# Three small reorderings in a Strassen MLP kernel: sums spread over three slots of a period, a reordered head, a last quarter by row tiles

## Chip, core and metric

The kernel runs on one core of one Trainium2 chip. The metric is the device time of one execution in microseconds. Every kernel below gave correct results. Times of one kernel agree within about 0.3% as a rule.

## The reference

```python
x (16, 512, 768)  w1 (768, 3072)  b1 (3072)  w2 (3072, 768)      # float32, random normal
y = x @ w1 + b1
y = 0.5 * y * (1 + erf(y / sqrt(2)))
return y @ w2
```

## The kernel before

Rows are taken in eight super-blocks of 1024. Each product is done by the Winograd form of Strassen's method: seven products of half-size blocks in place of eight, paid for by 16-bit sums of operands on VectorE. The second product of the last six super-blocks uses two levels of it. A super-block from the third on has twelve "periods" of the first product (`Unit1`), 4.53 us each, then seven of the second (`Unit3`), 6.93 us each. TensorE writes seven small products p1 to p7 into PSUM banks X, Y, Z and W; VectorE and ScalarE copy and add between the banks.

A period is one fixed order of work for the new unit `i` and the one before it, `j`. `fill(slot)` is where other work is pushed into the engines' in-order queues:

```python
def period(i, j, fill):
    ...                                    # [cut: the change from Unit1 to Unit3]
    p1(i); copy_xy(i)                      # X bank; ScalarE copies X to Y
    p7(j)                                  # onto j's Y bank; VectorE: Y add ("c22")
    fill(1)
    p5(i)                                  # W bank; ScalarE copies it out
    fill(2)
    p3(j)                                  # onto Z bank; VectorE: Z add ("c12")
    fill(3)
    p6(i)                                  # onto i's Y bank: needs copy_xy(i) done; then Y to Z copy
    j.right_done()                         # ScalarE: GELU of 1024 columns, needs the Z add
    fill(4)
    p4(j)                                  # ScalarE: GELU of the Y bank
    fill(5)
    p2(i)                                  # ScalarE: GELU of the X bank
    fill(6)
```

The sums that later products need wait in a queue. A slot takes from it as far as a budget in nanoseconds goes:

```python
def fill_mm1(sb, k, slot):                 # first product, super-blocks 2 to 7
    if slot == 1:
        ...                                # [cut: puts sums into the queue]
        sums(900)
    if slot == 4:
        sums(1500)
    ...                                    # [cut: loads of x, w1, w2; slot 5 loads only]
```

Since both queues of work are first-in-first-out, a sum put ahead of the Z add delays the Z add, and with it ScalarE's GELU and everything behind that.

The head (x tiles 4 to 7 are the bottom rows; `spin` is dummy matmuls):

```python
nc.gpsimd.tensor_copy(out=xh_of(0, 4)[:, 0:1], in_=xf[:, 1, 0:1])   # POOL waits for x tile 1 ...
for t in range(4, 8): load_x(0, t)                                   # ... before it asks for tiles 4 to 7
...
for t in range(4, 8):
    if t == 6: p2(first)
    transpose_pe(0, t)                     # TensorE transposes, ScalarE copies PSUM to SBUF
    spin(2 if t < 7 else 6)
    if t % 2:                              # sums S1, S2, A21, S4 of the top or the bottom half
        x_sums(0, soon, slice((t - 5) * P, (t - 3) * P))
        for k in range(4 if t < 7 else 2): soon.pop(0)[1]()
```

The end: in the last unit p4 goes onto the Y bank, VectorE adds 384 columns, one 192 KB store follows. The two sums that close the quarter before it (`c22_sum`, each with a 384 KB store) stand in slots 2 and 3 of the last full period.

## Time and profile before

| | before |
|---|---|
| time, median of 3 runs before the change | 865.12 us |
| profiled execution (865.78 us): span | 864.0 us |
| PE busy; LDWEIGHTS busy | 99%; 65% |
| 6310 matmuls at their usual spacing | 844.6 us |
| stretched spacing after the first 20 us | 8.7 us |
| last matmul's start to the end | 4.6 us |

"Spacing" is from the start of one matmul to the start of the next: 216 ns for 512 columns, 82 ns for 192, taken as the median of the trace. A "gap" below is what one spacing has beyond that. Gaps are the right measure here: the Trainium skill ("Perfetto Trace Analysis", Identifying the Most-Contended Engine) says that matmul busy share does not tell how close a kernel is to its limit, since matmuls are pipelined.

The timeline of the kernel before in a first-product period (columns: start us, busy us, engine, line, operation, output<-input, shapes, count, and in brackets idle time before it and what ended it). L179 is a sum, L562 the Z add, L386 and L391 GELUs, L528 the copy of X to Y.

```profile
593.11 1.21 DVE L179 TENSOR_TENSOR arena<-arena 128x512 f16<-128x512 f16 x3
...
594.24 0.68 DVE L562 TENSOR_TENSOR arena<-bZ,arena 128x512 f32<-128x512 f32 x1
...
595.49 1.15 ACT L386 ACTIVATE arena<-arena,b1t 128x1024 f16<-128x1024 f32 x1
...
597.11 0.69 ACT L391 ACTIVATE arena<-bX,b1t 128x512 f16<-128x512 f32 x1
...
597.68 0.60 ACT L528 COPY bY<-bX 128x512 f32<-128x512 f32 x1
...
598.34 1.46 PE L370 MATMUL bY<-arena 128*128 128x512 f16 x6
```

Three sums of slot 1 hold the Z add up to 594.24; ScalarE then works in a row to 598.28, and p6 starts at 598.34, with a gap of 275 ns. The timeline of the kernel before at the turn from the first product to the second and behind it. L535 is the Y add, L572 the "Z-bank add" of the second product (Y to Z), L462 its matmuls.

```profile
495.28 1.49 DVE L179 TENSOR_TENSOR arena<-arena 128x768 f16<-128x768 f16 x3
...
498.01 0.69 DVE L535 TENSOR_TENSOR arena<-bY,arena 128x512 f32<-128x512 f32 x1 [1.25 <-PE bY L370]
...
499.75 6.99 DVE L179 TENSOR_TENSOR arena<-arena 128x256 f16<-128x256 f16 x18
...
506.25 2.16 PE L462 MATMUL bY<-arena 128*128 128x192 f16 x24
...
509.17 0.57 DVE L572 TENSOR_TENSOR bZ<-bY,arena 128x384 f32<-128x384 f32 x1
...
517.05 0.56 DVE L572 TENSOR_TENSOR bZ<-bY,arena 128x384 f32<-128x384 f32 x1
...
517.66 1.15 PE L462 MATMUL bY<-arena 128*128 128x192 f16 x12 [0.35 <-DVE bZ L572]
```

VectorE idles 1.25 us before the Y add at 498.01, then has 18 sums to do.

The head of the kernel before, in its timeline: ScalarE's GELU and two transpose copies, the first bottom sum, p5 of the first unit, and p7 of the second unit, from which on the periods run steadily.

```profile
14.38 0.69 ACT L391 ACTIVATE arena<-bX,b1t 128x512 f16<-128x512 f32 x1 [0.26 <-PE bX L370]
...
14.96 1.49 ACT L296 COPY arena<-bT 128x768 f16<-128x768 f16 x2
...
16.48 1.62 DVE L179 TENSOR_TENSOR arena<-arena 128x768 f16<-128x768 f16 x3 [0.24 <-ACT arena L296]
...
17.10 0.81 PE L370 MATMUL bW<-arena 128*128 128x512 f16 x3 [0.42 <-DVE arena L179]
...
24.18 0.81 PE L370 MATMUL bY<-arena 128*128 128x512 f16 x3
```

Its last stretch (L179 with f32 are the two closing sums, L487 and L493 issue stores, L504 is the last add):

```profile
853.66 0.95 DVE L179 TENSOR_TENSOR arena<-arena 128x768 f32<-128x768 f32 x1
...
854.67 2.84 SPq L487 DMA_DIRECT2D out_dram<-arena  x4
...
858.45 1.15 PE L462 MATMUL bY<-arena 128*128 128x192 f16 x12
...
859.64 0.56 DVE L504 TENSOR_TENSOR arena<-bY,arena 128x384 f32<-128x384 f32 x1 [0.43 <-PE bY L462]
860.23 0.37 SPq L493 DMA_DIRECT2D out_dram<-arena  x1
```

### The profile page before, as it was taken

The page shows a single profiled execution, that of the slowest core. Times are in us where ns is not written, and L with a number is a line of the kernel's source. Part 1 is how long each engine was busy: PE and PEld are TensorE (multiplying, and loading weights), DVE is VectorE, ACT ScalarE, POOL GpSimd, SP SyncE. Part 2 cuts the span into 40 slices and gives each one's busy share as a digit, 9 for nine tenths or more (in the row PEclk, how much of TensorE's full clock was granted, in tenths as well). Part 3 has the DMA queues.
Part 4 walks back from the last instruction along what each step waited for, and adds up shares of the span by engine and source line. Part 5 has one row for each costly group of instructions (what it writes and reads, how often), then busy time and mean ns, then how long its engine had stood idle before and what let it go on. Part 6 is the DMA issues. An engine that isn't in the chain of part 4 may idle for free.

```text
span 864.0 us, 16201 instructions
## 1 busy us (share of the span) xinstructions
PE 853.0 (99%) x6310; PEld 560.9 (65%) x6310; DVE 653.7 (76%) x1106; ACT 420.6 (49%) x682; POOL 80.4 (9%) x131
## 2 busy tenths in 40 slices
PE   8999999999999999999999999999999999999997
PEld 4444445666544798448974499645995469944797
DVE  5765677656446998569976799667996689947997
ACT  5777762111178512874137732577216771277511
POOL 5111100000100001100020000200002100010000
PEclk9999999999999999999999999999999999999999
DMA  9987895659989698996989889897998959967397
GB/s 228 213 228 104 234 187 192 236 170 269 228 211 322 191 326 309 267 282 217 326 291 279 246 268 330 275 278 214 303 344 255 345 142 321 348 222 257 110 293 280
DMA packets 143249, 219.03 MB, mean 254 GB/s; under 512 B 61676, under 2 KB 84132, under 8 KB 143172
## 3 DMA queue, kind: packets, MB, share of 16 engines
q1 hardware_dynamic: 117952, 180.62, 66.1%
q0 software_dynamic: 25184, 37.36, 20.6%
q8 instruction: 49, 0.80, 0.4%
q14 instruction: 28, 0.23, 0.1%
q10 hardware_dynamic: 36, 0.01, 0.0%
HBM read 180.30 MB, written 47.87 MB: 264 GB/s over the span
## 4 chain that ended last, share of the span: by engine, by line
PE 82%; DVE 12%; issue 2%; DMA 2%; ACT 1%; SPq 0%; DVEq 0%; ACTq 0%
PE bY L370 21%; PE bX L370 14%; PE bY L462 10%; DVE arena L179 8%; PE bW L370 7%; PE bZ L370 6%; PE bX L462 6%; PE bY L410 5%; PE bX L410 4%; PE bZ L462 3%; PE bW L462 3%; PE bZ L410 2%; PE bW L410 2%; DMA arena<-w1s 1%; DVE bZ L572 1%
## 5 line engine op out<-in xcount | busy, mean ns | idle before, releaser
L179 DVE TENSOR_TENSOR arena<-arena 128x768 f16<-128x768 f16 (+4 forms) x620 | 393.8, 664 | 12.5 <-DMA arena<-arena 3.0
L370 PEld LDWEIGHTS <-arena 128*128 128x128 f16 x2016 | 196.3, 98 | 232.8 <-issue 3.5
L462 PEld LDWEIGHTS <-arena 128*128 128x128 f16 x3528 | 292.1, 98 | 12.6 <-issue 4.2
L370 PE MATMUL bY<-arena 128*128 128x512 f16 x864 | 218.9, 379 | 0.6
L535 DVE TENSOR_TENSOR arena<-bY,arena 128x512 f32<-128x512 f32 (+1 forms) x104 | 70.8, 681 | 149.6 <-PE bY L370 100.0
L528 ACT COPY bY<-bX 128x512 f32<-128x512 f32 (+1 forms) x146 | 80.3, 550 | 127.9 <-DVE arena L504 90.5
L370 PE MATMUL bX<-arena 128*128 128x512 f16 x576 | 141.5, 379 | 0.6 <-DMA arena<-w1s 0.6
L462 PE MATMUL bY<-arena 128*128 128x192 f16 x1512 | 139.8, 246 | 2.1 <-DVE bZ L572 2.1
L386 ACT ACTIVATE arena<-arena,b1t 128x1024 f16<-128x1024 f32 x96 | 110.3, 1149 | 57.5 <-DVE arena L562 57.5
L547 ACT COPY arena<-bW 128x512 f32<-128x512 f32 (+1 forms) x146 | 80.7, 553 | 95.5 <-PE bW L462 44.2
L410 PEld LDWEIGHTS <-arena 128*128 128x128 f16 x672 | 65.8, 98 | 44.2
L462 PE MATMUL bX<-arena 128*128 128x192 f16 x1008 | 92.0, 246 | 0.4
L562 DVE TENSOR_TENSOR arena<-bZ,arena 128x512 f32<-128x512 f32 (+1 forms) x104 | 70.5, 678 | 24.1 <-PE bZ L370 17.8
L370 PE MATMUL bW<-arena 128*128 128x512 f16 x288 | 77.8, 379 | 0.4 <-DVE arena L179 0.4
L370 PE MATMUL bZ<-arena 128*128 128x512 f16 x288 | 77.8, 379 | 0.0
L391 ACT ACTIVATE arena<-bX,b1t 128x512 f16<-128x512 f32 x96 | 65.3, 681 | 7.8 <-PE bX L370 7.8
L487 POOL DMA_DIRECT2D out_dram<-arena x42 | 30.5, 728 | 397.9 <-DVE arena L558 290.2
L391 ACT ACTIVATE arena<-bY,b1t 128x512 f16<-128x512 f32 x96 | 64.6, 673 | 0.0
L284 POOL DMA_DIRECT2D arena<-in_x_dram x60 | 32.3, 543 | 275.7 <-DMA arena<-arena 195.8
L577 DVE COPY bZ<-bY 128x512 f32<-128x512 f32 (+1 forms) x68 | 46.5, 683 | 6.7 <-PE bY L370 0.5
L410 PE MATMUL bY<-arena 128*128 128x384 f16 x288 | 49.6, 326 | 0.0
L462 PE MATMUL bW<-arena 128*128 128x192 f16 x504 | 49.0, 246 | 0.1
(41 smaller groups left out, 331.1 us busy)
## 6 DMA issues: line engine op xcount, KB each, us to landing
arena<-w2s SPq DMA_DIRECT2D x294, 288.0 KB, 4.6
arena<-w1s SPq DMA_DIRECT2D x72, 672.0 KB, 6.0
out_dram<-arena POOLq DMA_DIRECT2D x42, 384.0 KB, 5.1
w2s<-arena SPq DMA_DIRECT2D x49, 288.0 KB, 4.0
arena<-in_x_dram POOLq DMA_DIRECT2D x60, 192.0 KB, 6.8
w1s<-arena SPq DMA_DIRECT2D x12, 672.0 KB, 8.0
out_dram<-arena SPq DMA_DIRECT2D x21, 384.0 KB, 3.2
arena<-in_w_dram POOLq DMA_DIRECT2D x17, 384.0 KB, 8.1
```

The costliest lines, as they stand in the source:

```text
L179: nc.vector.tensor_tensor(out=o, in0=a, in1=b, op=op)
L284: nc.gpsimd.dma_start(out=xhs[t], in_=xr[:, sb * 8 + t, :])
L370: nc.tensor.matmul(out=dst[:, 0:RH], lhsT=w1_op(self.wt, slot)[:, c, :], rhs=a[:, c, :], start=first and c == 0, stop=c == self.C - 1, ski ...
L386: nc.scalar.activation(out=self.G[1][:, hi, :, :], in_=self.tmp, func=GELU, bias=b1t[:, 2 * hi + 1:2 * hi + 2])
L391: nc.scalar.activation(out=self.G[0][:, hi, row, :], in_=bank[:, 0:RH], func=GELU, bias=b1t[:, 2 * hi:2 * hi + 1])
L410: nc.tensor.matmul(out=dst[:, 0:N2], lhsT=a, rhs=w[:, :, c, :], start=first and c == 0, stop=c == self.C - 1, skip_group_check=True)
L462: nc.tensor.matmul(out=dst[:, t * N4:(t + 1) * N4], lhsT=a, rhs=w[:, c, :], start=first and c == 0 and t == 0, stop=c == NQ - 1, skip_grou ...
L528: nc.scalar.copy(out=bY[u.g % 2][:, 0:u.F], in_=bX[u.g % 2][:, 0:u.F])
L535: nc.vector.tensor_tensor(out=u.c22(), in0=bY[u.g % 2][:, 0:u.F], in1=w[:, 0:u.F], op=ADD)
L547: nc.scalar.copy(out=w[:, 0:u.F], in_=bW[:, 0:u.F])
L562: nc.vector.tensor_tensor(out=u.c12(), in0=bZ[:, 0:u.F], in1=w[:, 0:u.F], op=ADD)
L577: nc.vector.tensor_copy(out=bZ[:, 0:u.F], in_=bY[u.g % 2][:, 0:u.F])
```

## The change

Its intent: fewer sums ahead of the Z add; x's bottom rows asked for sooner and used sooner; a shorter piece of work behind the last matmul. The core of the diff, in three parts (cut: signatures that only pass the new arguments on).

```diff
 # --- sums ---
-                sums(900)
+                sums(500)              # slot 1
             if slot == 4:
                 sums(1500)
+            if slot == 5:
+                sums(500)

 # --- head ---
-        nc.gpsimd.tensor_copy(out=xh_of(0, 4)[:, 0:1], in_=xf[:, 1, 0:1])
+        nc.gpsimd.tensor_copy(out=xh_of(0, 4)[:, 0:1], in_=xf[:, 0, 0:1])
+        top, bottom = slice(0, 2 * P), slice(2 * P, RH)
         for t in range(4, 8):
-            if t == 6:
-                p2(first)
-            transpose_pe(0, t)
-            spin(2 if t < 7 else 6)
+            transpose_pe(0, t, nc.vector.tensor_copy if t == 5 else nc.scalar.copy)
             if t % 2:
-                x_sums(0, soon, slice((t - 5) * P, (t - 3) * P))
-                for k in range(4 if t < 7 else 2):
-                    soon.pop(0)[1]()
+                x_sums(0, soon, top if t == 5 else bottom, (0, 1))     # S1, S2 first
+                flush(soon)
+            if t < 7:
+                spin(2)
+        p2(first)
+        spin(3)
+        for r in (top, bottom):
+            x_sums(0, soon, r, (2,))
+        flush(soon)
+        for r in (top, bottom):
+            x_sums(0, soon, r, (3,))
-            on_act = isinstance(u, Unit3) or ...
+            on_act = u.g == 0 or isinstance(u, Unit3) or ...           # first unit's Y-to-Z copy by ScalarE
                 # [cut: both S4 sums are moved behind two sums of the next w1]

 # --- tail ---
+            def last(self, banks):                 # p4 of the last unit
+                for t in range(2):
+                    self.mm(4, banks[t], True, 0, self.C, (t,))
+                    o = self.dst[:, 1, t, 0, :]
+                    tt(o, banks[t][:, t * N4:(t + 1) * N4], o, ADD)
+                    nc.sync.dma_start(out=orr[:, self.sb * 8 + 2 + t, N2:N2 + N4], in_=o)
                 # [cut: the add of the Y bank moves up behind p7]
-                if sb + 1 == nsb and slot in (2, 3):
-                    units3[5].c22_sum(slot - 2)
+                if sb + 1 == nsb and slot in (1, 2):
+                    units3[5].c22_sum(slot - 1)
```

More of the change, by code (lines that the diff above doesn't have):

```diff
@@ L290, in transpose_dma, with transpose_pe @@
             nc.sync.dma_start_transpose(out=xT_of(sb, t), in_=xhs[t])
-        def transpose_pe(sb, t):
+        def transpose_pe(sb, t, copy=nc.scalar.copy):
             for kc in range(2 * KQ):
@@ L295, in transpose_pe @@
                                     identity=ident[:])
-            nc.scalar.copy(out=xT_of(sb, t), in_=bT[t % 2][:])
+            copy(out=xT_of(sb, t), in_=bT[t % 2][:])
         def blocks(sb):
@@ L300, in blocks, with x_sums @@
             return [XT[:, a, c:c + KQ, :] for a in range(2) for c in (0, KQ)]
-        def x_sums(sb, q, r=slice(0, RH)):
+        def x_sums(sb, q, r=slice(0, RH), ks=range(4)):
             A11, A12, A21, A22 = [a[:, :, r] for a in blocks(sb)]
@@ L305, in x_sums @@
             n = KQ * len(range(RH)[r])
-            later(n, lambda: tt(S1, A21, A22, ADD), q)
-            later(n, lambda: tt(S2, S1, A11, SUB), q)
-            later(n, lambda: tt(A21, A11, A21, SUB), q)
-            later(n, lambda: tt(S4, A12, S2, SUB), q)
+            ops = ((S1, A21, A22, ADD), (S2, S1, A11, SUB), (A21, A11, A21, SUB), (S4, A12, S2, SUB))
+            for k in ks:
+                later(n, lambda k=k: tt(*ops[k]), q)
         def g_sum(k, U, c0=0, c1=NH, q=None):
@@ L448, in __init__, with mm @@
                 self.alloc = lambda: None
-            def mm(self, q, dst, first, c0, c1):
+            def mm(self, q, dst, first, c0, c1, ts=(0, 1)):
                 A = OPERAND[self.p]
@@ L455, in mm @@
                 for c in range(NQ):
-                    for t in range(2):
+                    for t in ts:
                         r = slice(t * P, (t + 1) * P)
@@ L463, in mm @@
                                          rhs=w[:, c, :],
-                                         start=first and c == 0 and t == 0,
+                                         start=first and c == 0 and t == ts[0],
                                          stop=c == NQ - 1, skip_group_check=True)
                 load_ring(self.sb, n + RING)
+            def last(self, banks):
[4 more added lines that the diff above has]
+                    nc.sync.dma_start(out=orr[:, self.sb * 8 + 2 + t, N2:N2 + N4], in_=o)
             def quarter(self, o, r, h):
@@ L509, in finish @@
             def finish(self):
-                if self.ends:
-                    self.store_quarter(1, 0)
-                elif self.p in (2, 3, 4):
+                if not self.ends and self.p in (2, 3, 4):
                     self.store(0)
@@ L542, in p7 @@
                 u.store_quarter(1, 1)
+                u.left_done(1, bY[u.g % 2])
         def p5(u):
@@ L564, in p4 @@
         def p4(u):
+            if isinstance(u, Unit3) and u.ends:
+                u.last(bX)
+                return
             u.mm(4, bY[u.g % 2], False, 0, u.C)
@@ L569, in p6 @@
             u.mm(6, bY[u.g % 2], False, 0, u.C)
-            on_act = isinstance(u, Unit3) or (isinstance(u, Unit1) and u.sb >= ONE and u.g % 2)
+            on_act = u.g == 0 or isinstance(u, Unit3) or (isinstance(u, Unit1) and u.sb >= ONE and u.g % 2)
             if isinstance(u, Unit3) and u.add is not None:
@@ L718, in fill_a @@
             if slot == (1 if pos < at[1, 0] else 4) and pos + 1 < len(seq) and seq[pos + 1][0] == 0:
-                s4 = [soon.pop(1)] if pos == 0 else []
+                s4 = [soon.pop(0), soon.pop(0)] if pos == 0 else []
                 prep_wt(seq[pos + 1][1])
-                soon[3:3] = s4
+                soon[2:2] = s4
             if slot == 4:
```

## The prediction

> **What bounds it now.** The TensorE stream. The page shows PE busy 99% of the 864.0 us span at clock 0.999; VectorE is at 76%. In the timeline matmuls start 216 ns apart for 512 columns and 82 ns for 192; at such cadences 6310 matmuls take 844.6 us. So about 20 us is all that any reordering can touch: 4.9 us of stretched issue in the first 20 us, 8.7 us of later gaps, and head wait and tail.
>
> **First products (six super-blocks from 237 us).** PE's gaps end on ScalarE's copy of the X bank into the Y bank (about 197 ns at 371, 580 and 787 us; 277 ns at 598 and 806; 284 ns at 290, 498 and 706). The copy is late because two 16-bit sums (0.52 us each; three of 0.42) stand in slot 1 before VectorE's add of the Z bank, which then starts 0.4 to 0.5 us after its product ended; bank copy, three GELUs (1.15, 0.68, 0.68) and the X copy follow in a row. After: slot 1 holds one sum, the others go behind it or into slot 5, where VectorE idles 0.15 to 1.3 us. These eight gaps (2.0 us) should close. One 1024-column sum (0.68) also moves ahead of the batch of 18 at the change to the second product, so that batch ends earlier: the 187 and 101 ns gaps at 401/609/817 and 403/611/819 should close (0.85). Not touched: 511 ns before each "Z bank" add of the second product, six times (same order there), and the 730 ns wait for w1 at 387.
>
> **Head.** p5 of the first unit starts at 17.10, released by VectorE's last S1 sum, itself behind the last transpose copy (ScalarE busy with a GELU, two copies 14.96 to 16.45). After: that GELU comes after the copies, one copy goes to VectorE (estimate 0.9 us), sums stand S1, S2 first. I expect p5 near 16.3. Asking for x about 0.95 us sooner buys little: x tiles land at 11.57, 12.52, 13.51, 14.42, one each microsecond behind x and w1 already queued. The Trainium skill ("DMA: Bandwidth & Descriptors", Issuing engines are not separate DMA queues) says that all issuers share the same 16 engines; the trace agrees, about 380 KB/us read throughout. VectorE then is continuous (sums from 15.7, add, Z copy) until p7 of the second unit, near 23.6 instead of 24.18. Gain 0.55 us.
>
> **Tail.** Last matmul ends at 859.6; a 0.56 us add, then a 192 KB store 860.23 to 862.99. After: add of 192 columns (estimate 0.36), store of half the size; Most of the 2.8 us store is fixed. Gain 0.4 us.
>
> **Sum.** 2.85 + 0.55 + 0.4 = 3.8 us; I discount a little for gaps that move: 861.5 us, range 860.0 to 863.3. Chances: faster by over 2% 0.00, same 0.99, slower 0.01.
>
> **What would show it.** Gaps at the eight places and the two pairs gone, Z-bank add starting at its product's end; 511 ns gaps still there; first unit's p5 at 16.3; x bottom tiles landing no more than 0.4 us sooner; last store issued some 0.2 us earlier after the last matmul. Total PE excess after 20 us: 8.7 down to 5.5.
>
> **What would make it wrong.** Earlier x requests delaying w1's or x's first loads (p1 beyond 11.3); sums in slot 5 delaying the next Y add or Z copy, opening new gaps; waits for w1 reloads, which vary by run.

## More of the kernel before

From the page of the kernel before: its first line, the busy line, and the chain of waits that ended last, by engine.

```profile
span 864.0 us, 16201 instructions
...
PE 853.0 (99%) x6310; PEld 560.9 (65%) x6310; DVE 653.7 (76%) x1106; ACT 420.6 (49%) x682; POOL 80.4 (9%) x131
...
PE 82%; DVE 12%; issue 2%; DMA 2%; ACT 1%; SPq 0%; DVEq 0%; ACTq 0%
```

For 12% of the span the chain runs through VectorE, although VectorE is idle a quarter of the time.

## The result, and the profile after

The changed kernel took 858.08 us (857.61 to 858.25, 4 runs), the kernel before 865.15 us (4 runs): ratio 0.9915, 95% interval 0.9898 to 0.9933. (A ratio is the mean time of one kernel's fast runs over that of the other's of the same rounds, so it is not quite the ratio of the medians quoted.) That is "same" at a threshold of 2%, but it lies below the range that I gave: 7.1 us were gained, I had forecast 3.6.

The page of the kernel after, same lines:

```profile
span 856.2 us, 16201 instructions
...
PE 850.1 (99%) x6307; PEld 560.7 (65%) x6307; DVE 653.8 (76%) x1108; ACT 421.2 (49%) x682; POOL 80.6 (9%) x131
...
PE 97%; DMA 2%; ACT 0%; DVE 0%; SPq 0%; issue 0%
```

PE is busy 99% as before, and LDWEIGHTS rises only from 65% to 65.5% of a shorter span; what changed is the chain: VectorE's share of it fell from 12% to 0%. Where the 7.7 us between the two spans (863.97 and 856.25 us) came from, read off the two traces (the kernel before was profiled in an execution 0.6 us slower than its median; a gap of 39 ns near the end closed too):

| place | before | after | gained, us |
|---|---|---|---|
| eight gaps on the copy of X to Y (195 to 285 ns) | 1.99 us | 0.02 | 1.97 |
| three pairs of gaps at the turn to the second product (about 187 and 101 ns) | 0.86 | 0 | 0.86 |
| six gaps on the Z-bank add | 3.06 | 0.56 | 2.50 |
| two gaps at 45 and 49 us | 0.18 | 0 | 0.18 |
| p7 of the second unit starts at | 24.18 | 22.80 | 1.38 |
| last matmul's start to the end | 4.62 | 3.86 | 0.75 |
| wait for a reload of w1, at 387 us | 0.73 | 0.74 | 0 |

The first two rows, 2.83 us together, are what I had forecast (2.85). The third row was forecast as nothing, and the head and the tail came out larger.

The period of the kernel after at the same place in the schedule as the first one shown of before (L567 is the Z add, L390 a GELU, L532 the copy of X to Y):

```profile
589.43 0.41 DVE L179 TENSOR_TENSOR arena<-arena 128x512 f16<-128x512 f16 x1
...
589.76 0.68 DVE L567 TENSOR_TENSOR arena<-bZ,arena 128x512 f32<-128x512 f32 x1
...
592.64 0.69 ACT L390 ACTIVATE arena<-bX,b1t 128x512 f16<-128x512 f32 x1
...
593.21 0.60 ACT L532 COPY bY<-bX 128x512 f32<-128x512 f32 x1
...
594.03 1.46 PE L369 MATMUL bY<-arena 128*128 128x512 f16 x6
```

One sum, not three, stands ahead of the Z add, and the copy is over 0.22 us before p6 could start. The turn to the second product in the kernel after (L539 is the Y add, L580 the Z-bank add):

```profile
491.86 2.09 DVE L179 TENSOR_TENSOR arena<-arena 128x768 f16<-128x768 f16 x4
...
494.90 0.69 DVE L539 TENSOR_TENSOR arena<-bY,arena 128x512 f32<-128x512 f32 x1 [0.95 <-ACT arena L390]
...
496.64 6.26 DVE L179 TENSOR_TENSOR arena<-arena 128x256 f16<-128x256 f16 x17
...
502.86 2.14 PE L461 MATMUL bY<-arena 128*128 128x192 f16 x24
...
505.34 0.57 DVE L580 TENSOR_TENSOR bZ<-bY,arena 128x384 f32<-128x384 f32 x1
...
513.22 0.56 DVE L580 TENSOR_TENSOR bZ<-bY,arena 128x384 f32<-128x384 f32 x1
...
513.83 1.15 PE L461 MATMUL bY<-arena 128*128 128x192 f16 x12
```

Four sums instead of three run ahead of the Y add, in time in which VectorE was idle, and 17 are left behind it. From p6's first matmul to the first Z-bank add it is now 2.48 us, before it was 2.92; the second one holds TensorE up by 0.43 us less, too: its gap is 83 ns instead of 512.

The head of the kernel after, same lines as before, with ScalarE's Y-to-Z copy (L583):

```profile
14.51 0.80 ACT L296 COPY arena<-bT 128x768 f16<-128x768 f16 x1 [0.18 <-PE bT L294]
...
15.34 4.35 DVE L179 TENSOR_TENSOR arena<-arena 128x768 f16<-128x768 f16 x10 [0.87 <-ACT arena L296]
15.95 0.81 PE L369 MATMUL bW<-arena 128*128 128x512 f16 x3 [0.19 <-DVE arena L179]
...
17.44 0.57 ACT L583 COPY bZ<-bY 128x512 f32<-128x512 f32 x1
...
22.80 0.81 PE L369 MATMUL bY<-arena 128*128 128x512 f16 x3
```

A single copy stands between the last x tile and the first bottom sum, and ten sums then run on VectorE without a pause. The end of the kernel after (L472 issues the two halves of the last store):

```profile
846.00 0.95 DVE L179 TENSOR_TENSOR arena<-arena 128x768 f32<-128x768 f32 x1
...
847.01 3.27 SPq L493 DMA_DIRECT2D out_dram<-arena  x4
...
851.48 1.15 PE L461 MATMUL bX<-arena 128*128 128x192 f16 x12
...
852.17 0.85 DVE L179 TENSOR_TENSOR arena<-bX,arena 128x192 f32<-128x192 f32 x2
...
852.73 1.00 SPq L472 DMA_DIRECT2D out_dram<-arena  x2
```

### The profile page after: what moved, and what is told of

It is laid out like the page before. It is cut to its first block, busy times and chain, and to the rows that moved or that the text cites. A ratio compares the mean times of both kernels' runs of the same rounds, so it can differ in the third digit from the quotient of the medians.

```text
span 856.2 us, 16201 instructions
## 1 busy us (share of the span) xinstructions
PE 850.1 (99%) x6307; PEld 560.7 (65%) x6307; DVE 653.8 (76%) x1108; ACT 421.2 (49%) x682; POOL 80.6 (9%) x131
## 4 chain that ended last, share of the span: by engine, by line
PE 97%; DMA 2%; ACT 0%; DVE 0%; SPq 0%; issue 0%
PE bY L369 21%; PE bY L461 15%; PE bX L369 14%; PE bX L461 10%; PE bW L369 7%; PE bZ L369 7%; PE bY L409 5%; PE bZ L461 5%; PE bW L461 5%; PE bX L409 4%; PE bZ L409 2%; PE bW L409 2%; DMA arena<-w1s 1%; DMA arena<-in_x_dram 1%; PE bT L294 0%; ACT arena L296 0%
## 5 line engine op out<-in xcount | busy, mean ns | idle before, releaser
L539 DVE TENSOR_TENSOR arena<-bY,arena 128x512 f32<-128x512 f32 (+1 forms) x104 | 70.8, 681 | 144.7 <-PE bY L369 88.7
L532 ACT COPY bY<-bX 128x512 f32<-128x512 f32 (+1 forms) x146 | 80.3, 550 | 125.0 <-DVE arena L510 87.7
L567 DVE TENSOR_TENSOR arena<-bZ,arena 128x512 f32<-128x512 f32 (+1 forms) x104 | 70.7, 680 | 25.5 <-PE bZ L369 18.4
L390 ACT ACTIVATE arena<-bX,b1t 128x512 f16<-128x512 f32 x96 | 65.4, 681 | 7.5 <-PE bX L369 7.5
L390 ACT ACTIVATE arena<-bY,b1t 128x512 f16<-128x512 f32 x96 | 64.7, 674 | 0.0
L461 PE MATMUL bZ<-arena 128*128 128x192 f16 x504 | 48.5, 246 | 0.0
```

The lines of the kernel that those rows point to most:

```text
L390: nc.scalar.activation(out=self.G[0][:, hi, row, :], in_=bank[:, 0:RH], func=GELU, bias=b1t[:, 2 * hi:2 * hi + 1])
L461: nc.tensor.matmul(out=dst[:, t * N4:(t + 1) * N4], lhsT=a, rhs=w[:, c, :], start=first and c == 0 and t == ts[0], stop=c == NQ - 1, skip_ ...
L532: nc.scalar.copy(out=bY[u.g % 2][:, 0:u.F], in_=bX[u.g % 2][:, 0:u.F])
L539: nc.vector.tensor_tensor(out=u.c22(), in0=bY[u.g % 2][:, 0:u.F], in1=w[:, 0:u.F], op=ADD)
L567: nc.vector.tensor_tensor(out=u.c12(), in0=bZ[:, 0:u.F], in1=w[:, 0:u.F], op=ADD)
```

## The experiments

Eighteen kernels ran. All outputs are right. "Before" is the kernel before on the same chip.

### One part at a time, and one slot

`sums_only`, `head_only` and `tail_only` are the kernel before with one of the three parts of the diff. `no5_last` is the changed kernel with

```diff
-            if slot == 5:
+            if slot == 5 and k < NH - 1:
                 sums(500)
```

> The kernel before with only the sums spread over three slots. Backlog theory (VectorE enters the second product with one 0.68 us sum less to do, and carries no lateness to the Z-bank add): the six gaps of 511 ns shrink to about 80, the copy gaps (197, 277, 284 ns) and the 187/102 pairs close; time 5.0 to 5.6 us below the kernel before. Rival, the prediction's sum: the 511 ns gaps stay, 2.9 us below. Rival, that head or tail fed the gain: under 2 us below.

> The kernel before with only the head part. If the head is worth what the two traces show: p7 of the second unit near 22.8 us instead of 24.18, time 1.2 to 1.6 us below the kernel before; x's third tile and w1 land about 0.5 us sooner. Rival, that the sooner landing is a run-to-run matter: p7 near 23.3 to 23.6, 0.5 to 0.9 us below. The 511 ns gaps stay.

> The kernel before with only the last quarter by row tiles and the earlier closing sums. From the two traces: last matmul to end 3.8 us instead of 4.6, so 0.8 us below the kernel before (0.85 with the 39 ns gap closed). Prediction's estimate: 0.4 us. Nothing else moves.

> The changed kernel, with no sums in slot 5 of the twelfth (last) first-product period alone. Backlog theory: the moved 1024-column sum goes back behind the last Y add, VectorE is 0.68 us later into the second product, and TensorE loses about 0.6 us more in each of six super-blocks: 3.2 to 4.0 us above the changed kernel, the Z-bank gap back to 500 ns or more; the copy gaps stay closed. Rival (the lighter slot 1 of all periods did it): within 0.6 us of the changed kernel.

| kernel | median us (range) | before | ratio, 95% interval | gaps after 20 us in the trace |
|---|---|---|---|---|
| sums_only | 859.58 (859.04 to 860.86) | 864.73 | 0.9942 [0.9928, 0.9956] | 3.4 us (before: 8.7) |
| head_only | 866.48 (864.19 to 867.77) | 864.73 | 1.0015 [1.0001, 1.0028] | 8.2 us |
| tail_only | 865.23 (863.59 to 865.47) | 864.73 | 0.9997 [0.9985, 1.0010] | 8.6 us |
| no5_last | 861.98 (861.66 to 862.34) | 864.73 | 0.9965 [0.9953, 0.9978] | 6.8 us |

The sums alone give 5.2 us, with every Z-bank gap at 81 to 87 ns: the prediction's 2.9 us for this part is refuted. `no5_last` costs 3.9 us against the changed kernel: the copy gaps stay closed but for one of 175 ns at 388 us, while the pairs (about 188 and 102 ns, now in every super-block) and a Z-bank gap of 511 to 591 ns are back. So the third row of the table hangs on the one sum that slot 5 of the last period takes, not on the lighter slot 1.

Head and tail alone were misses: their traces show what was expected of them (p7 of the second unit at 23.1 us; 3.86 us from the last matmul to the end), yet the times do not.

### That slot alone; head and tail on top of the sums; a first attempt at a better version

`only5_last` is the kernel before with nothing but

```diff
+            if slot == 5 and k == NH - 1:
+                sums(500)
```

`sums_head` and `sums_tail` leave one part out of the change. `best` is the changed kernel with

```diff
-                sums(500)                              # slot 5
+                sums(1000 if k == NH - 1 else 500)
-                if 3 <= k < 11: transpose_dma(...)      # slot 3: ahead of the w1 and w2 loads
+                # the same in slot 5, behind them
-                    nc.sync.dma_start(...)              # both halves of the last store
+                    (nc.sync if t else nc.scalar).dma_start(...)
```

> The kernel before with one thing added: a slot of 500 ns of sums at the end of the twelfth first-product period, which pulls one 1024-column sum (0.68 us) ahead of the last Y add in each of six super-blocks. Backlog theory: the copy gaps (197, 277, 284 ns) stay, since slot 1 is as before; of the Z-bank gap and the 187/102 pair together 0.5 to 0.7 us per super-block go, so 3.0 to 4.2 us below the kernel before. Rival (light slot 1 did it): under 0.6 us below.

> The changed kernel without the tail part. Traces of the parts: head 0.6 us (p7 of the second unit comes 8.9 us after x's last tile lands instead of 9.1 to 9.8), so 858.6 to 859.1. If the parts interact as their separate runs seemed to (head alone 1.7 us above the kernel before): above 860.

> The changed kernel without the head part. The trace of the tail part alone says 0.75 us, so 858.6 to 859.0 here. If the parts interact (tail alone was no faster than the kernel before): above 859.4.

> A version meant to beat both: the changed kernel, with 1000 instead of 500 ns of sums in slot 5 of the last first-product period (closes the six gaps of 80 ns: 0.45 us), the x transposes of a period issued behind the loads of w1 and w2 (the 737 ns wait for w1 goes, and others like it in runs not profiled), and the first half of the last store issued by ScalarE (the second half is issued about 0.2 us sooner). Expected 856.4 to 857.4, against 858.1; if the w1 wait is the DMA engines' and not the queue's order, 857.4 to 857.8.

| kernel | median us (range) | before | ratio, 95% interval |
|---|---|---|---|
| only5_last | 861.22 (860.84 to 864.86) | 864.74 | 0.9959 [0.9946, 0.9972] |
| sums_head | 858.66 (857.73 to 862.54) | 864.74 | 0.9935 [0.9921, 0.9948] |
| sums_tail | 858.67 (858.26 to 860.00) | 864.74 | 0.9934 [0.9922, 0.9946] |
| best | 858.05 (857.63 to 860.08) | 864.74 | 0.9930 [0.9918, 0.9942] |

`only5_last` moves one sum of 0.68 us in each of six super-blocks and gains 3.5 us. Its copy gaps are all there (195 to 286 ns), the pairs are gone, the Z-bank gaps are 138 and twice 74 ns in odd super-blocks and none in even ones. With `no5_last` this shows the backlog theory from both sides: VectorE enters the second product with a backlog of sums, and that backlog is what TensorE later waits for. (The profiled execution of `only5_last` was its slowest, 864.86 us; it has three waits for w1, 3.3 us in all, and such waits vary by execution.) Its timeline in an even super-block:

```profile
714.56 2.14 PE L462 MATMUL bY<-arena 128*128 128x192 f16 x24
...
716.75 0.57 DVE L572 TENSOR_TENSOR bZ<-bY,arena 128x384 f32<-128x384 f32 x1
...
724.63 0.56 DVE L572 TENSOR_TENSOR bZ<-bY,arena 128x384 f32<-128x384 f32 x1
...
725.45 1.15 PE L462 MATMUL bY<-arena 128*128 128x192 f16 x12
```

The first Z-bank add starts 2.19 us after p6's first matmul, where it was 2.92 us in the kernel before, and the second one is over 0.26 us before the matmul that needs it.

On top of the sums, head and tail are worth 0.9 us each in the medians, and 1.3 to 1.5 us together (858.08 and, later, 858.32 against 859.58). These medians come from different calls and the intervals of the ratios overlap, so the times alone do not show it.

`best` did not beat the changed kernel. The 80 ns gaps closed, but gaps of 408, 407 and 406 ns opened in the odd super-blocks. There VectorE is idle only 0.16 us before the last Y add (0.95 us in even ones), so the extra sum (512 columns, 0.42 us) delayed the last Z add. The timeline of `best` at 392 us: the Z add, then ScalarE's chain up to the Y-to-Z copy (L583), which is over at 397.25, and the matmul onto that Y bank.

```profile
393.52 0.68 DVE L567 TENSOR_TENSOR arena<-bZ,arena 128x512 f32<-128x512 f32 x1
...
394.24 1.15 ACT L385 ACTIVATE arena<-arena,b1t 128x1024 f16<-128x1024 f32 x1 [2.53 <-DVE arena L567]
...
396.75 0.50 ACT L583 COPY bZ<-bY 128x384 f32<-128x384 f32 x1
...
397.30 1.15 PE L461 MATMUL bY<-arena 128*128 128x192 f16 x12 [0.24 <-DMA arena<-w2s]
```

The trace puts the wait down to a load of w2, but that load landed at 396.72; the copy, done 0.05 us before the matmul, fits better. The wait for w1 stayed too (808 ns, over at 385.46). In the changed kernel that load was issued at 375.44 and landed at 385.41, 10.0 us later, where the median of w1 reloads is 5.8 us. `best` does not clear the order of SyncE's queue, though: it moved the transposes behind the w1 load of the same period, but they still stand ahead of the next period's. Its load was issued at 376.23, 0.10 us after the end of a transpose that had waited for a tile of x until 374.88. All 20 traces point the same way. TensorE waits for this load in twelve; in each of them a transpose that had waited for x stands right ahead of it, and the load was issued 4.77 to 6.14 us after the w1 load before it. In seven of the other eight no transpose waited, and the load came 4.53 us after, one period (in the eighth 4.96, with no wait). So late x tiles, passed on by SyncE's in-order queue, are the likely cause; no run takes the transposes out of the way, so this is not shown. Once issued, the load took 8.9 to 10.0 us in the twelve and 6.6 to 9.4 in the eight.

### A second attempt, and three parts of the head

`best2` gives slot 5 its second sum only where the trace has room, keeps the transposes where they were and ScalarE's issue of the first half store:

```diff
-                sums(500)                              # slot 5
+                sums(1000 if k == NH - 1 - sb % 2 else 500)
```

`x_on_tile1`, `copy5_act` and `bz_dve` are the changed kernel with one line of the head put back: `xf[:, 1, 0:1]`; `nc.scalar.copy` for all four tiles; no `u.g == 0`.

> The changed kernel with two additions: slot 5 may take 1000 ns of sums in one period of each super-block where the trace shows VectorE idle before the Y add for more than the extra sum (the twelfth period of even super-blocks, 0.95 us; the eleventh of odd ones, 0.62 us); and ScalarE issues the first half of the last store. The six 80 ns gaps close without the 408 ns gaps that the first attempt opened in odd super-blocks: 857.4 to 857.7, against 858.1. Should odd super-blocks show new gaps again: 858.0 or more.

> The changed kernel, but the bottom rows of x are again asked for only when x's second tile is there. If the transfers are bound by the shared DMA engines (the prediction): the last x tile lands where it does in the other runs, 13.6 to 14.4 us, and p7 of the second unit starts 8.9 us after it. If asking sooner counts: last tile at 14.6 or later.

> The changed kernel with the sixth tile's transposed copy back on ScalarE. ScalarE then has copies of 0.8 us at 12.8 and is free again by 13.7, before the last tile is transposed at 14.5: p7 of the second unit stays 8.9 us after the last tile's landing (within 0.1). Rival, that VectorE's copy is a part of the head's gain: 9.2 us or more after it.

> The changed kernel with the first unit's Y-to-Z copy back on VectorE (0.70 us). VectorE works without a pause from the last x tile to the second unit's p7, so that p7 moves to 9.4 to 9.6 us after the last tile's landing, instead of 8.9. Rival (VectorE has room): 9.0 or less.

`best2`: 857.52 us (856.82 to 860.04), before 865.15, ratio 0.9914 [0.9898, 0.9930]; none of the six gaps is left in its trace, and no new ones but for waits for w1 (682 and 244 ns). ScalarE's issue bought nothing: the second half of the last store was issued 0.2 us sooner after the last matmul's start than in the changed kernel, but took 2.29 us to land in place of 2.07, so the end came 3.87 us after that start, before 3.86. For the head, the useful measure is the time from the landing of x's last tile to p7 of the second unit:

| trace | last x tile lands, us | p5 of the first unit after it | p7 of the second unit after it |
|---|---|---|---|
| before | 14.42 | 2.68 | 9.76 |
| tail_only, only5_last, sums_tail | 13.57, 14.83, 14.31 | 2.56 to 2.59 | 9.64 to 9.66 |
| sums_only (a tile landed late; ScalarE was free) | 14.27 | 2.04 | 9.12 |
| changed kernel | 13.91 | 2.04 | 8.88 |
| head_only, sums_head, no5_last, best, best2 | 13.76 to 14.23 | 2.03 to 2.04 | 8.88 to 8.89 |
| x_on_tile1 (858.89 us, one run) | 14.32 | 2.04 | 8.88 |
| copy5_act (857.29 us, one run) | 13.91 | 2.04 | 8.88 |
| bz_dve (859.47 us, one run) | 13.62 | 2.04 | 9.48 |

`bz_dve` is 0.60 us worse: VectorE is the limit there, and giving the copy to ScalarE is worth that. `copy5_act` shows that the copy by VectorE buys nothing. `x_on_tile1` came out inside the band expected if the shared DMA engines bind (13.6 to 14.4), near its upper end; over all traces, x's last tile lands at a median of 13.91 us when asked for after tile 0 (13 traces) and 14.32 us after tile 1 (7 traces), but single values overlap (13.54 to 14.90 against 13.57 to 14.83).

### The tail, the head again, and the better version again

`tail_one` keeps the last product in one piece:

```diff
-                for t in range(2):
-                    self.mm(4, banks[t], True, 0, self.C, (t,))
-                    ...                                # add and store of 192 columns each
+                self.mm(4, banks[0], True, 0, self.C)
+                o = self.quarter(self.dst, 1, 0)
+                tt(o, self.bank(banks[0]), o, ADD)
+                self.store_quarter(1, 0)
```

`head_again` is `head_only`, `after_again` the changed kernel, `best2_again` is `best2`.

> The changed kernel, but the last quarter's final product is summed, added and stored in one piece (384 columns wide, one 192 KB store). If the split gave the tail: from the last matmul's start to the end 4.5 to 4.6 us, as before, instead of 3.86. If only the narrower add counts (0.2 us) and the store's time is fixed, as the prediction had it: 4.0 to 4.2.

> The head part alone, a second time. If waits for w1 reloads come and go by execution: times spread again over 864 to 868, and the trace of a slow execution shows one to three gaps of 0.4 us or more released by the w1 load, while p7 of the second unit stays 8.9 us after the last x tile. If the head part itself costs time: all runs above 865 and a gap at the same place in both traces.

> The changed kernel again, for the same chip as best2_again: 857.6 to 858.3, with single runs later where a w1 load is late.

> The further version again: 0.4 to 0.6 us below the changed kernel of the same call, by the six gaps of 80 ns. If waits for w1 take it back: within 0.2 us.

`tail_one` (861.80 us, one run) takes 3.94 us from the last matmul's start to the end, the split 3.86: the split into row tiles buys 0.08 us, and both of my expectations were wrong. What differs from before lies in the stores ahead: the last store takes 2.09 us from issue to landing, in the kernel before 2.77 us for the same 192 KB.

| kernel | median us (range) | before | ratio, 95% interval |
|---|---|---|---|
| head_again | 864.64 (863.27 to 865.05) | 864.93 | 0.9991 [0.9979, 1.0003] |
| after_again | 858.32 (857.38 to 859.05) | 864.93 | 0.9921 [0.9908, 0.9933] |
| best2_again | 858.42 (856.46 to 861.68) | 864.93 | 0.9922 [0.9905, 0.9939] |

The head part alone is not slower after all, 0.3 us below here. In this trace w1's second half landed at 11.97 us, not at about 10, and p7 came 9.76 us after the last x tile in place of 8.9; in `tail_one` it landed at 13.71 and p7 came 11.7 us after. None of seven traces with the old request had it later than 10.70; two of thirteen with the new one did by over 1 us. That is the risk that the prediction named, but two of thirteen do not prove it. What held up the slow executions (up to 867.8) is not seen, since none of them was profiled.

`best2` is not shown to be faster than the changed kernel: in one call their medians differ by 0.1 us, though its gaps of about 80 ns are gone (0.54 us in the trace of `after_again`). In that trace the wait for w1 at 384 us is 1.33 us; in the changed kernel's it is 0.98, in other traces anything from 0 to 1.1 at that place.

### The closing sums

`c22_old` is the changed kernel with `slot in (2, 3)` and `slot - 2` for the closing sums; `c22_only` is the kernel before with `slot in (1, 2)` and `slot - 1`.

> The changed kernel with the two closing sums back in the slots where they stood. If the earlier sums gave the tail: the last store takes 2.7 us again from issue to landing, last matmul to end 4.3 to 4.6 us, and the 39 ns gap is back. If the split gives the same by itself: 3.9 us.

> The kernel before with only the two closing sums one slot earlier. If they gave the tail: last matmul to end 3.9 to 4.0 us, the last store 2.1 us from issue to landing, the 39 ns gap gone. If not: 4.5 to 4.6 us.

| kernel | last store, issue to landing | last matmul's start to the end | 39 ns gap |
|---|---|---|---|
| before | 2.77 us | 4.62 us | yes |
| c22_only | 2.09 us | 3.94 us | no |
| changed kernel | 2.07 us (half the size) | 3.86 us | no |
| c22_old | 2.60 us (half the size) | 4.51 us | 37 ns |

This settles it: the closing sums, one slot earlier, give 0.68 us of the tail's 0.75, because their stores are out of the way sooner (read from one trace of each kernel; the times of the tail alone do not show it). In the kernel before the last four stores land 1.12, 0.59, 1.12 and 0.57 us after the one ahead of each (1.12 us for 384 KB, 0.57 to 0.59 for 192 KB): they stand in a queue, and the last store waits for those ahead. Even in `c22_only` it landed 0.58 us after the one ahead, so 0.68 us is the least that it waited before. (Times: 860.70 and 864.50 us, one run each; `c22_old` had a wait of 2.5 us for w1.)

## Why the prediction was wrong

- **The copy gaps and the pairs**: right. Forecast 2.0 and 0.85 us, measured 1.97 and 0.86, by the mechanism given: fewer sums ahead of the Z add, and a shorter batch.
- **"Not touched: 511 ns before each 'Z bank' add of the second product, six times (same order there)"**: this step failed, and it is the larger part of the miss, 2.50 us. The order of instructions there is the same, but VectorE enters it behind TensorE, and stays behind: I had read the 0.1 us idle in front of the first Z-bank add (509.17) as VectorE having caught up, while p6 had been done about 1.7 us earlier. A queue that never empties carries a lead of 0.68 us at its start on to every later wait. `only5_last` and `no5_last` show it. I had even listed that lead, and credited it to the nearest pair of gaps alone.
- **Head**: the mechanism was right in part (p5 at 16.3 forecast, 15.95 measured; p7 near 23.6, measured 22.80), the size was off: 0.55 us forecast, 1.38 between the two traces, and the two small gaps at 45 and 49 us (0.18) besides. Of the 1.38, 0.88 are the order of work after the last tile (9.76 to 8.88), where I had 0.6 or less. `bz_dve` gives 0.60 of the 0.88 to the first unit's Y-to-Z copy, which the change moves to ScalarE and the prediction does not name; all else in the new order is worth 0.28 (9.76 to 9.48). The other 0.51 is x's last tile landing sooner in this pair of traces, more than the 0.4 us that I allowed; the medians of all traces differ by 0.4, and single values overlap. "Asking for x about 0.95 us sooner buys little" is therefore neither shown nor refuted; I had counted nothing for it.
- **"One copy goes to VectorE (estimate 0.9 us)"**: 0.56 us in the trace, and worth nothing (`copy5_act`).
- **Tail**: "Most of the 2.8 us store is fixed. Gain 0.4 us": this step failed too. The split gave 0.08 us; 0.68 us came from the closing sums, which I had passed over. Little of the store's time depends on its size (half of it took 2.07 us in place of 2.09, and 2.60 in place of 2.77), but it was not fixed: at least 0.68 us of the 2.77 was waiting behind other stores.
- **The w1 wait**: named and left alone, rightly; 0.73 and 0.74 us in the two traces.

The cause is settled for the sums and the tail. Open is what makes w1 reloads late (a transpose held up ahead of them in SyncE's queue is likely, from the traces, but was not tested), whether the earlier x request sometimes delays w1's first load, and why head and tail alone do not show in the times.

## What to carry to other kernels

When an engine runs behind its consumer, follow its queue back to the last place where it was truly idle: one item moved into that idle time shortens every wait downstream until the queue empties, so moving 0.68 us once per super-block gained more than closing the visible gaps. Check "caught up" against the end of the work it waits for, not against a small idle figure. At the end of a kernel, look at the stores queued ahead of the last one before splitting the last one.

## What the Trainium skill lacked or had wrong

- "DMA: Bandwidth & Descriptors", Anatomy of one DMA, gives for one DMA that GpSimd issues about 2.0 us fixed plus bytes at 436 GB/s. Carried over to these stores, which SyncE issues, that makes an estimate of 2.45 us for 192 KB. The runs show 2.09 us with two stores not yet landed ahead of it and 2.77 us with three: a sum for a single DMA has no term for the queue ahead, which here was the larger lever. Stores in the queue landed 1.12 us apart for 384 KB, about 350 GB/s.
- The same page, Issuing engines are not separate DMA queues, says that transfers of all issuers interleave on the same engines. The traces agree (in the kernel before, the last tiles of x, asked for by GpSimd, land 0.9 to 1.0 us apart, as w1's two halves, asked for by SyncE, do just ahead of them). The page does not say what an earlier request costs the transfers beside it: in two of thirteen traces with the earlier request for x, w1's second half landed at 11.97 and 13.71 us instead of about 10, though that the request did this is not shown.
- No page says how long a 672 KB reload takes beside other transfers: its median is 5.7 to 6.5 us in these traces, and every trace has some of over 9 us, at several places of the kernel.
- "Perfetto Trace Analysis", Identifying the Most-Contended Engine: that matmul busy share is no measure holds (99% before and after); the LDWEIGHTS busy share that it names instead moved in the right direction, 65% to 65.5%, but is too coarse for a gain of 0.85%. The spacing of matmul starts against its median showed every gap in the table above.
